# Layer 0's output product in a written order, with heads made ready two ahead, weights' low parts on two engines, and h scaled by its norm ahead of a plain transpose

## The chip, the cores and the metric

The kernel runs on one core of one Trainium2 chip. The metric is the device time of one execution in microseconds (us); the time of a kernel is the median of its runs. Five engines work side by side, each through its own instructions in order: TensorE (PE, with its weight loads PEld), VectorE (DVE), ScalarE (ACT), GpSimd (POOL) and SyncE (SP), which issues nearly all transfers. Engines wait for each other through semaphores. Matrix products are made by PE from on-chip memory (SBUF) into PSUM; DVE and ACT read both, POOL is used on SBUF alone.

## The reference

The model has two layers over 256 context tokens and 512 latent tokens of width 1024. Layer 0 mixes by a bidirectional gated delta rule with 16 value heads of width 128, layer 1 by grouped-query attention. What the change touches is the end of layer 0, the gated residual, and the norm ahead of layer 1:

```python
def finish(o, z):
    b, h, l, dv = o.shape
    o = rms_norm(jnp.transpose(o, (0, 2, 1, 3)), o_norm_g).astype(z.dtype)
    return (o.reshape(b, l, DN_VAL_DIM) * jax.nn.silu(z)) @ w_out
...
        h_lat = h_lat + gate[:, None] * y_lat
        if need_ctx:
            h_ctx = h_ctx + gate_c * y_ctx
...
        u_lat = rms_norm(h_lat, norm_g[i]) * (1.0 + scale[:, None]) + shift[:, None]
        u_ctx = rms_norm(h_ctx, norm_g[i]) * (1.0 + scale_c) + shift_c
```

Here `rms_norm(x, g)` is x over the root of the mean of its squares (plus 1e-6), times g.

## The kernel before

**Tiles.** The 768 tokens are six tiles of 128 rows: 0 and 1 the context, 2 to 5 the latents. Layer 0 leaves the mixer's result in `O[t]`, one tile of 128 x 16 x 128 for each token tile. Products are made with operands split in two: a high part rounded to the matrix engine's fp32r and a low part, the rest. Each product is three matmuls (`PASS`: high by high, high by low, low by high). The high part of a weight or an activation is a copy by ACT, the low part a subtraction by DVE or POOL.

**The scan.** Layer 0's recurrence takes some 50 steps x, which end shortly before 791 us. Beside its last steps run small pieces of work: `square_o` sums the squares of a head of `O[t]` on ACT, and `scale_pieces` makes the reciprocal root from them on DVE in pieces between steps (by a shift, a magic constant and three Newton steps) and then scales `O[t]` on POOL, four heads an instruction (L863). Tiles 0, 1 and 5 are treated so.

**The output product.** `out_group(gi)` runs twice. Group 0 has the token tiles 0, 1, 5, group 1 the tiles 4, 3, 2 (`GROUPS`). A group runs over the 16 heads, so there are 32 units. `out_prep` makes a head ready: it loads the 128 rows of `w_out` of the head (L870), copies the high part on ACT (L871), subtracts the low part on POOL as one 128x1024 instruction (L872), loads the gate z, transposes the three tiles of `O` on PE (L895), multiplies by z and the norm's weight on DVE (L898), and makes the high part y on ACT (L900) and the low part on DVE (L901). The unit is then 3 tiles x 2 halves x 3 passes = 18 matmuls of 128x512 (L1138) that add up over the heads in six PSUM tiles `po`. `out_prep` of a head is written one unit ahead of its products. The pool `fw` has two buffers for w, wh, wl, z and y.

In group 0, at heads 2, 5 and 8, the squares and the scale of the tiles 4, 3, 2 are made: 16 `square_o` on ACT and `scale_o`, whose last instruction scales a whole tile on POOL (L827). In group 1, at heads 3, 5, 7 and 9, the key/value weights of layer 1 (`wkv`) are loaded and split.

**The end of a group.** For each of its three tiles and two halves DVE multiplies the sum by the gate (`gy`, L1143, four buffers), POOL adds it to `h_t` (L1144), and ACT sums the squares (L1145). `norms1` makes the reciprocal root on DVE and from it, on ACT, a diagonal matrix `diag1[t]` (L1167). `u_block(k, ...)` turns block k of 128 columns: a matmul of `h_t` with the diagonal (L1174) transposes and scales in one, DVE applies the affine map of layer 1 (L1176), ACT and DVE make the two parts (L1177, L1178). `u_block` for the context is written beside `kv_block` (L1240), the key/value products, for the latents behind it.

**What sets the order.** Up to this point a scheduler orders the instructions of each engine from the program, from priorities and from when it thinks operands are ready; `issue_after` keeps an instruction behind a named one. From the blocks of the latents on (`manual_schedule`) PE, DVE and ACT run in the order in which the code is written; POOL and SP stay with the scheduler.

## Time and profile before

| | |
|---|---|
| time, median of 3 runs | 1297.53 us (1296.28 to 1298.45) |
| the profiled execution: its own time | 1297.93 us |
| the profiled execution: span from first to last instruction | 1296.2 us |
| mean granted TensorE clock | 0.966 of full speed |
| first and last product of the output stage (L1138) | 791.0 and 959.7 us |
| its 576 matmuls, in 32 units | 18 each |
| first and last `u_block` matmul (L1174) | 950.3 and 1001.8 us |

All times in the trace are of one profiled execution, counted from the first instruction. A row of a timeline gives start, duration, engine, line, operation, tiles and shape; in brackets stands the idle time of the engine ahead of the instruction and what ended it. A row of one line's summary gives the shortest, median and longest duration in ns and the first and last start. Matmuls are pipelined, so their durations overlap and the distance from one start to the next is what one costs.

### The profile page before, as it was taken

Reading aid. Unit: us, or ns where it says so; the run is one execution under the profiler, and the core shown is the slowest. Engines: PE = TensorE matmul, PEld = TensorE weight load, DVE = VectorE, ACT = ScalarE, POOL = GpSimd, SP = SyncE. Lnnn points to the kernel's source line nnn. Section 1 sums busy time; section 2 is a strip of 40 time slices with the busy share of each in tenths; the row PEclk is TensorE's granted clock in tenths of the full one; section 3 lists DMA queues with packets and bytes.
Section 4 is the critical chain, followed back from the end, with each engine's and each line's share of the span. In section 5 each row is a group of like instructions: output and inputs, shape, how many; then the busy total and the mean of one; then the engine's idle time right before and its main releaser. Section 6 shows DMA issues by size and latency. Waiting matters only on the chain.

```text
span 1296.2 us, 28116 instructions
## 1 busy us (share of the span) xinstructions
PE 1170.6 (90%) x10803; PEld 940.9 (73%) x10803; DVE 822.0 (63%) x1800; ACT 705.3 (54%) x1892; POOL 641.8 (50%) x503
## 2 busy tenths in 40 slices
PE   3999999999789898999999988897999787989996
PEld 1676778888678777887666655685787677878874
DVE  2688566777897466765888884754346456555535
ACT  3344336665476768963898874633332244545621
POOL 0121132169989998302665785675662234331540
PEclk9999999999899988999999999998999988989998
DMA  9366976355545597539799666454642021010233
GB/s 315 130 220 206 327 245 169 113 167 167 151 123 184 154 269 239 180 125 283 235 247 246 166 181 172 152 166 134 186 133 66 1 65 50 17 34 33 66 98 97
DMA packets 165351, 204.56 MB, mean 158 GB/s; under 512 B 13377, under 2 KB 114914, under 8 KB 164322
## 3 DMA queue, kind: packets, MB, share of 16 engines
q1 hardware_dynamic: 146402, 193.33, 49.0%
q10 hardware_dynamic: 18816, 9.44, 2.5%
q8 instruction: 85, 1.39, 0.4%
q14 instruction: 48, 0.39, 0.1%
HBM read 161.96 MB, written 40.67 MB: 156 GB/s over the span
## 4 chain that ended last, share of the span: by engine, by line
PE 54%; DVE 14%; POOL 9%; DMA 9%; ACT 8%; issue 4%; SPq 1%; ACTq 0%; DVEq 0%; POOLq 0%
PE ks L979 6%; PE g_q L335 5%; PE po L1138 5%; PE g_v L335 4%; PE g_z L335 4%; PE pg L1348 3%; PE su L1034 3%; PE po L1426 2%; PE g_k L335 2%; PE pg L1371 2%; PE pr L1004 2%; POOL wol L872 2%; POOL X L677 2%; PE pso L1445 2%; POOL tmp L676 2%
## 5 line engine op out<-in xcount | busy, mean ns | idle before, releaser
L987 POOL TENSOR_TENSOR S<-S,glb 128x512 f32<-128x512 f32 x88 | 90.1, 1047 | 112.5 <-PE ks L979 112.4
L1138 PE MATMUL po<-woh,y 128*128 128x512 f32 x384 | 127.8, 403 | 11.1 <-ACT y L900 8.3
L335 PE MATMUL g_v<-uh,wh 128*128 128x512 f32 (+1 forms) x256 | 91.5, 357 | 15.7 <-DVE sil_v L362 15.7
L872 POOL TENSOR_TENSOR wol<-wo,woh 128x1024 fp32r<-128x1024 f32 x32 | 76.3, 2390 | 52.7 <-ACT woh L871 52.4
L677 POOL TENSOR_TENSOR X<-X,tmp 128x62 f32<-128x62 f32 (+15 forms) x93 | 96.8, 1040 | 6.5
L979 PE MATMUL ks<-S,ckq 128*64 128x256 f32 x768 | 93.5, 385 | 3.4 <-ACT o L984 2.7
L357 DVE SCALAR_TENSOR_TENSOR acc_v<-g_v,cwv,acc_v 128x510 f32<-128x510 f32 (+3 forms) x128 | 74.4, 609 | 34.7 <-ACT acc_v L354 33.2
L335 PE MATMUL g_z<-uh,wh 128*128 128x512 f32 (+1 forms) x256 | 88.9, 347 | 4.6 <-DVE sil_v L362 4.5
L676 POOL TENSOR_TENSOR tmp<-L,X 128x62 f32<-128x62 f32 (+15 forms) x93 | 89.1, 958 | 6.9
L1138 PEld LDWEIGHTS po<-woh,y 128*128 128x128 f32 x384 | 71.6, 191 | 27.7 <-ACT y L900 9.2
L335 PE MATMUL g_v<-ul,wh 128*128 128x512 f32 (+1 forms) x256 | 90.0, 352 | 0.0
L335 PE MATMUL g_v<-uh,wl 128*128 128x512 f32 (+1 forms) x256 | 89.2, 349 | 0.0
L335 PE MATMUL g_z<-ul,wh 128*128 128x512 f32 (+1 forms) x256 | 87.4, 342 | 0.0
L335 PE MATMUL g_z<-uh,wl 128*128 128x512 f32 (+1 forms) x256 | 87.3, 341 | 0.0
L979 PEld LDWEIGHTS ks<-S,ckq 128*64 128x64 f32 x768 | 50.7, 136 | 42.6 <-ACT o L984 11.7
L1138 PE MATMUL po<-wol,y 128*128 128x512 f32 x192 | 77.6, 404 | 4.0 <-POOL wol L872 4.0
L317 POOL TENSOR_TENSOR wl_k<-w_k,wh_k 128x1024 fp32r<-128x1024 f32 x8 | 19.0, 2386 | 101.8 <-ACT wh_k L316 101.8
L335 PEld LDWEIGHTS g_v<-uh,wh 128*128 128x128 f32 x256 | 50.8, 198 | 22.5 <-DVE sil_v L362 16.4
L1397 ACT ACTIVATE pr<-s,nm,sq 128x768 f32<-128x768 f32 x32 | 31.8, 993 | 62.9 <-DVE nm L1394 62.4
L1348 PE MATMUL pg<-wq,uL 128*128 128x256 f32 x384 | 56.0, 293 | 5.0 <-ACT qj L1357 2.6
L1052 DVE TENSOR_TENSOR S<-su,S 128x512 f32<-128x512 f32 x88 | 56.5, 683 | 4.1 <-PE su L1034 2.9
L982 DVE SCALAR_TENSOR_TENSOR r<-ks,negV,cv 128x128 f32<-128x128 f32 x192 | 56.1, 343 | 3.3 <-PE ks L979 2.5
(370 smaller groups left out, 3384.6 us busy)
## 6 DMA issues: line engine op xcount, KB each, us to landing
aw<-in_ada_w SPq DMA_DIRECT2D x24, 1024.0 KB, 7.8
w<-in_dn_w_in SPq DMA_DIRECT2D x40, 512.0 KB, 4.4
wo<-in_dn_w_out SPq DMA_DIRECT2D x32, 512.0 KB, 3.3
cv<-v_d SPq DMA_DIRECT2D x80, 128.0 KB, 5.3
df<-gc_d SPq DMA_DIRECT2D x48, 128.0 KB, 2.8
z_d<-zs SPq DMA_DIRECT2D x16, 384.0 KB, 4.9
v_d<-vt ACTq DMA_DIRECT2D x16, 384.0 KB, 3.9
t_d<-Tt SPq DMA_DIRECT2D x6, 1024.0 KB, 4.8
```

The lines of the kernel that those rows point to most:

```text
L335: mm = T.matmul(pg_[:m, :n], w[:, k, :m], u[:, k, c0:c0 + n], start=k == 0 and n_ == 0, stop=k == KT - 1 and n_ == 2)
L357: V.scalar_tensor_tensor(acc[:, c0 + lo:c0 + hi], ps[:, lo + j - 2:hi + j - 2], cwv[:, j, ct:ct + 1], acc[:, c0 + lo:c0 + hi], ALU.mult, A ...
L676: E.tensor_tensor(tv, bcast(L[:, :, j + 1:, j], 3, j + 1), bcast(X[:, :, j, 0:j + 1], 2, n), ALU.mult)
L677: E.tensor_tensor(X[:, :, j + 1:, 0:j + 1], X[:, :, j + 1:, 0:j + 1], tv, ALU.subtract)
L872: G.tensor_tensor(wl, w, wh, ALU.subtract)
L979: T.matmul(ks[r0:r0 + 64, w], kq[:, w, slot(hh), r0:r0 + 64], St[hh][:, d], start=True, stop=True)
L982: V.scalar_tensor_tensor(r[:, 2 * j + i], ks[:, 0, i], negV[:, visit, t, h0 + i:h0 + i + 1], v[:, 2 * hh + i], ALU.mult, ALU.add)
L987: G.tensor_tensor(St[hh], St[hh], bcast(g_, 3, P), ALU.mult)
L1034: T.matmul(su[c0:c0 + 64, d ^ j, j], kt[r0:r0 + 64, 4 * j + p, c0:c0 + 64], vd[r0:r0 + 64, 2 * j:2 * j + 2], start=True, stop=True)
L1052: V.tensor_tensor(St[hh], raw(sj, 0, [[512 - 1024 * j, 2], [P, 2], [1, P]]), St[hh], ALU.add)
L1138: T.matmul(acc[j][nh], y[i][:, j, :], ww[k][:, nh * 512:(nh + 1) * 512], start=h == 0 and x == 0, stop=h == VH - 1 and x == 2)
L1348: T.matmul(pgq, uL[i][:, k, t * P:(t + 1) * P], wq[j][:, k], start=k == 0 and n_ == 0, stop=k == KT - 1 and n_ == 2)
```

## The change

From the output stage on, PE, DVE and ACT run in the written order (`manual_schedule` now opens ahead of the 32 units). The loop over the units `n` does, in this order: load z of head n+3 (three buffers); make y of head n+2 ready (three buffers); up to three pieces of `scale_pieces` for the tiles 4, 3, 2, which begin at the units 4, 7 and 10 and use the unused quarter of the transposes' PSUM tile; five squares of `O` on ACT until the 48 are done (units 0 to 9); in unit 20 the norm of group 0, in units 21 to 23 the scaling of its h by ACT, and from unit 24 on one context `u_block` in each; then the 18 products; the gated products at a group's end (`gy` with six buffers); in unit 4 the loads of h for group 0 and of the gate, in unit 10 those of h for group 1, each behind the next head's weight load; then the weights of head n+2, whose low part is now two halves of 512 columns, one by POOL and one by DVE; two additions to h in each of the units 16, 17 and 18; and the key/value weights as before.

`h_t` is now scaled in place by its norm, and `u_block` is a transpose with the identity in place of a product with a diagonal. At the end of group 1 POOL adds one half of each tile and DVE the other; the 8 context `kv_block` stand together, then the norm, then the scaling of tile 4 on ACT, tile 3 on DVE and tile 2 on ACT. `scale_o` is gone. In `scale_pieces`, which the scan uses too, the result of the shift is written to PSUM and no longer to SBUF.

```diff
-        V.tensor_single_scalar(y.bitcast(I32), f.bitcast(I32), 1, ALU.logical_shift_right)
-        V.tensor_scalar(y.bitcast(I32), y.bitcast(I32), -1.0, float(0x5F3759DF), ALU.mult, ALU.add)
+        V.tensor_single_scalar(sp.bitcast(I32), f.bitcast(I32), 1, ALU.logical_shift_right)
+        V.tensor_scalar(y.bitcast(I32), sp.bitcast(I32), -1.0, float(0x5F3759DF), ALU.mult, ALU.add)
...
+    def out_weights(n, shared=True):
...
         S.copy(wh, w)
-        G.tensor_tensor(wl, w, wh, ALU.subtract)
-        return wh, wl
+        c = 512 if shared else D
+        G.tensor_tensor(wl[:, :c], w[:, :c], wh[:, :c], ALU.subtract)
+        if shared:
+            V.tensor_tensor(wl[:, c:], w[:, c:], wh[:, c:], ALU.subtract)
+        weights[n] = wh, wl
...
+    def added(t, nh, gy, E):
+
+        c = slice(nh * 512, (nh + 1) * 512)
+        E.tensor_tensor(h_t[t][:, c], h_t[t][:, c], gy, ALU.add)
+        S.activation(gy, h_t[t][:, c], AF.Square, accum_out=hsq[:, ORDER.index(t), nh:nh + 1])
+        if t >= 2 and nh == 1:
+            dma(h_d[t - 2], h_t[t])
...
+    def normed(t, E):
+
+        r = hr[:, ORDER.index(t):ORDER.index(t) + 1]
+        if E is S:
+            S.activation(h_t[t], h_t[t], AF.Copy, scale=r)
+        else:
+            E.tensor_scalar(h_t[t], h_t[t], r, None, ALU.mult)
...
         for q, t in enumerate(tiles):
-            T.matmul(ps[:, q, :], h_t[t][:, k * P:(k + 1) * P], diag1[t], start=True, stop=True)
+            T.transpose(ps[:, q, :], h_t[t][:, k * P:(k + 1) * P], ident)
...
+    for n in range(len(units0)):
+        gi, h = units0[n]
...
+        if n + 3 < len(units0):
+            out_z(n + 3)
+        pt = out_y(n + 2) if n + 2 < len(units0) else None
+        for x in [x for x in chores if x <= n]:
+            for _ in range(3):
+                try:
+                    chores[x].send(pt[:, 3])
...
+        for t, h_ in squares[:5]:
+            square_o(t, h_)
+        squares = squares[5:]
+        if n == 20:
+            norms1(0, (pt[:, 3, 0:3], pt[:, 3, 64:67]))
+        if n in (21, 22, 23):
+            normed(ORDER[n - 21], S)
+        if n >= 24:
+            u_block(n - 24, 1, (0, 1), uC)
+        products0(n, acc)
+        if h == VH - 1:
+            late_adds = gated(gi, acc)
+        if n in (4, 10):
+            with tc.issue_after(w_at[n + 1]):
+                load_h(n // 10)
+                if n == 4:
+                    dma(gate0, gate_d[0])
+        if n + 2 < len(units0):
+            out_weights(n + 2)
+        if n in (16, 17, 18):
+            for x in range(2):
+                added(*late_adds.pop(0), G)
...
     for k in range(KT):
-        u_block(k, 1, (0, 1), uC)
         kv_block(k, (0, 1))
-    norms1((2, 3, 4, 5), "l")
-    manual = ExitStack()
-    manual.enter_context(tc.manual_schedule(engines={T.engine, V.engine, S.engine}))
+    norms1(1, room("hl", 3))
+    for t, E in ((4, S), (3, V), (2, S)):
+        normed(t, E)
```

What this moves on the engines is shown at three places. A name ends in a number that is the program's own count; `y_7_0` is the high or low part of y made for head 7 of group 0, `woh` and `wol` are the weight's two parts, `pt` the transposed tiles.

The first is DVE in group 0, in the middle of the norm of one tile of `O`. Before, with `fo` and `rs` (both in SBUF) as its scratch:

```order
L901 TENSOR_TENSOR y_7_0_10623<-pt_0_10615,y_7_0_10622 128x384
L898 SCALAR_TENSOR_TENSOR pt_0_10653<-pt_0_10653,og,z_0_10650 128x128 x2
L824 TENSOR_TENSOR fo<-oss,or_7093 128x16
L174 TENSOR_SCALAR fo<-fo 128x16
L175 TENSOR_SCALAR rs_12_10572<-fo 128x16
L185 TENSOR_SCALAR rs_12_10572<-rs_12_10572 128x16
L188 SCALAR_TENSOR_TENSOR rs_12_10573<-rs_12_10572 128x16
L189 TENSOR_TENSOR rs_12_10573<-rs_12_10573,fo 128x16
```

After, one unit there, from the low part of y to DVE's half of the weight's low part:

```order
L902 TENSOR_TENSOR y_9_0_10672<-pt_0_10664,y_9_0_10671 128x384
L847 TENSOR_SCALAR pt_0_10664<-oy 128x16
L848 TENSOR_TENSOR fo<-pt_0_10664,rq 128x16
L828 COPY pt_0_10664<-oss 128x16
L829 TENSOR_TENSOR pt_0_10664<-pt_0_10664,rq 128x16
L830 COPY ow<-pt_0_10664 128x16
L832 COPY pt_0_10664<-ow 128x16
L833 TENSOR_TENSOR pt_0_10664<-pt_0_10664,rq 128x16
L834 TENSOR_SCALAR fo<-pt_0_10664 128x16
L836 TENSOR_SCALAR pt_0_10664<-fo 128x16
L837 TENSOR_SCALAR oy<-pt_0_10664 128x16
L867 TENSOR_TENSOR wol_0_10714<-wo_0_10712,woh_0_10713 128x512
```

The small steps now go in pieces through PSUM (`pt`), each in a fixed place behind the low part of y, and a 128x512 subtraction closes the unit on DVE.

The second place is POOL at the switch of the groups. Before:

```order
L872 TENSOR_TENSOR wol_1_10984<-wo_1_10982,woh_1_10983 128x1024
L1144 TENSOR_TENSOR h_10293<-h_10293,gy_0_11020 128x512
L1144 TENSOR_TENSOR h_10293<-h_10293,gy_1_11024 128x512
L1144 TENSOR_TENSOR h_10294<-h_10294,gy_0_11028 128x512
L1144 TENSOR_TENSOR h_10294<-h_10294,gy_1_11032 128x512
L872 TENSOR_TENSOR wol_1_11081<-wo_1_11079,woh_1_11080 128x1024
L1144 TENSOR_TENSOR h_10298<-h_10298,gy_0_11036 128x512
L1144 TENSOR_TENSOR h_10298<-h_10298,gy_1_11040 128x512
L872 TENSOR_TENSOR wol_1_11119<-wo_1_11117,woh_1_11118 128x1024
```

After:

```order
L865 TENSOR_TENSOR wol_1_11051<-wo_1_11049,woh_1_11050 128x512
L1136 TENSOR_TENSOR h_10293<-h_10293,gy_0_11088 128x512
L865 TENSOR_TENSOR wol_1_11102<-wo_1_11100,woh_1_11101 128x512
L1136 TENSOR_TENSOR h_10293<-h_10293,gy_1_11090 128x512
L1136 TENSOR_TENSOR h_10294<-h_10294,gy_0_11092 128x512
L1136 TENSOR_TENSOR h_10294<-h_10294,gy_1_11094 128x512
L1136 TENSOR_TENSOR h_10298<-h_10298,gy_0_11096 128x512
L1136 TENSOR_TENSOR h_10298<-h_10298,gy_1_11098 128x512
L865 TENSOR_TENSOR wol_1_11147<-wo_1_11145,woh_1_11146 128x512
```

The three weights are those of heads 0, 1 and 2 of group 1 (units 16, 17, 18). The second moved ahead of all additions but one; five additions now stand between it and the third.

The third place is ACT at the same switch. Before:

```order
L1145 ACTIVATE gy_0_11020,hsq<-h_10293 128x512
L1145 ACTIVATE gy_1_11024,hsq<-h_10293 128x512
L1145 ACTIVATE gy_0_11028,hsq<-h_10294 128x512
L871 CAST woh_1_11118<-wo_1_11117 128x1024
L1145 ACTIVATE gy_1_11032,hsq<-h_10294 128x512
L1145 ACTIVATE gy_0_11036,hsq<-h_10298 128x512
L900 CAST y_1_1_11095<-pt_1_11088 128x384
L1145 ACTIVATE gy_1_11040,hsq<-h_10298 128x512
```

After:

```order
L901 CAST y_1_1_11066<-pt_1_11059 128x384
L863 CAST woh_1_11101<-wo_1_11100 128x1024
L901 CAST y_2_1_11123<-pt_1_11116 128x384
L863 CAST woh_1_11146<-wo_1_11145 128x1024
L1137 ACTIVATE gy_0_11088,hsq<-h_10293 128x512
L1137 ACTIVATE gy_1_11090,hsq<-h_10293 128x512
L901 CAST y_3_1_11166<-pt_1_11159 128x384
L863 CAST woh_1_11189<-wo_1_11188 128x1024
```

The y of unit 17 (`y_1_1`) stood behind five squares of h; now it and the y and weight of unit 18 stand ahead of the first square.

More of the change, by code (lines that the diff above doesn't have):

```diff
@@ L881, in backbone, with out_z, out_y @@
     units0 = [(gi, h) for gi in range(2) for h in range(VH)]
-    ready, first_w = {}, {}
-    def out_prep(gi, h, pt=None):
-        wh, wl = first_w.pop(h) if gi == 0 and h < 2 else out_weights(gi, h)
-        z = fw.tile([P, 3 * P], F32, tag="z", name=f"z{h}_{gi}")
+    ys, weights, zs, w_at = {}, {}, {}, {}
+    def out_z(n):
+        gi, h = units0[n]
+        z = fw.tile([P, 3 * P], F32, tag="z", name=f"z{h}_{gi}", bufs=3)
         c = 0
-        for c0, n in ZCOLS[gi]:
-            dma(z[:, c:c + n], z_d[h, :, c0:c0 + n])
-            c += n
+        for c0, m in ZCOLS[gi]:
+            dma(z[:, c:c + m], z_d[h, :, c0:c0 + m])
+            c += m
+        zs[n] = z
+    def out_y(n, pt=None):
+        gi, h = units0[n]
+        z = zs.pop(n)
         if pt is None:
@@ L898, in out_prep @@
             V.scalar_tensor_tensor(pj, pj, og, raw(z, off, [[st_, 2], [1, 64]]), ALU.mult, ALU.mult)
-        y = [fw.tile([P, 3, P], F32R, tag=f"y{i}", name=f"y{i}_{h}_{gi}") for i in range(2)]
-        ready["copy"] = S.copy(y[0], pt[:, :3]).ins
+        y = [fw.tile([P, 3, P], F32R, tag=f"y{i}", name=f"y{i}_{h}_{gi}", bufs=3) for i in range(2)]
+        S.copy(y[0], pt[:, :3])
         V.tensor_tensor(y[1], pt[:, :3], y[0], ALU.subtract)
-        ready[gi, h] = y, (wh, wl)
+        ys[n] = y
+        return pt
     with tc.tile_pool(name="psC", bufs=2, space=PSUM, reuse_waits="tile") as pcx:
@@ L1075, in backbone @@
                 if x in (45, 46):
[L1076 removed]
+                    out_weights(x - 45, False)
+                    out_z(x - 45)
         for _, g_ in chores:
@@ L1099, in backbone @@
     gate0 = fw.tile([P, 2, D], F32, tag="gate0", name="gate0", bufs=1)
-    with tc.issue_after(mark[1]):
-        dma(gate0, gate_d[0])
     def room(nm, n):
@@ L1139, in out_group, with products0, gated @@
+    ORDER = [t for g_ in GROUPS for t, _, _ in g_]
+    def products0(n, acc):
+        gi, h = units0[n]
+        y, ww = ys.pop(n), weights.pop(n)
+        for j in range(3):
+            for nh in range(2):
+                for x, (i, k) in enumerate(PASS):
+                    T.matmul(acc[j][nh], y[i][:, j, :], ww[k][:, nh * 512:(nh + 1) * 512], start=h == 0 and x == 0, stop=h == VH - 1 and x == 2)
+    def gated(gi, acc):
+        out_ = []
         for j, (t, _, _) in enumerate(GROUPS[gi]):
@@ L1178, in u_block @@
         V.tensor_tensor(dst[1][:, k], pv, dst[0][:, k], ALU.subtract)
-    with tc.issue_after(mark[0]), tc.issue_after(mark[1]):
-        load_h(0)
-    out_group(0)
-    norms1((0, 1), "c")
-    load_h(1)
-    out_group(1)
+    manual = ExitStack()
+    manual.enter_context(tc.manual_schedule(engines={T.engine, V.engine, S.engine}))
+    with tc.issue_after(mark[1]):
+        out_z(2)
+    chores = {4: scale_pieces(4, 1), 7: scale_pieces(3, 1), 10: scale_pieces(2, 1)}
+    for g_ in chores.values():
+        next(g_)
@@ new lines, in backbone @@
+    squares = [(t, h) for t in (4, 3, 2) for h in range(VH)]
+    late_adds = []
+    for n in range(len(units0)):
+        gi, h = units0[n]
+        if h == 0:
+            acc = [[pf.tile([P, 512], F32, tag=f"po{j}{nh}", name=f"po{gi}{j}{nh}") for nh in range(2)] for j in range(3)]
+        if n + 3 < len(units0):
[5 more added lines that the diff above has]
+                    chores[x].send(pt[:, 3])
+                except StopIteration:
+                    chores.pop(x)
+                    break
+        for t, h_ in squares[:5]:
[20 more added lines that the diff above has]
+                added(*late_adds.pop(0), G)
+        if gi == 1 and h in (3, 5, 7, 9):
+            k0 = h - 3
+            w = fw.tile([P, D], F32, tag="w", name=f"w1kv_{k0}")
+            wv = w.rearrange("p (k n) -> p k n", n=512)
+            dma(wv, wa[:, k0:k0 + 2, 1024:1536])
+            S.copy(wkv[0][:, k0:k0 + 2], wv)
+            G.tensor_tensor(wkv[1][:, k0:k0 + 2], wv, wkv[0][:, k0:k0 + 2], ALU.subtract)
@@ L1186, in backbone @@
+    for t, nh, gy in late_adds:
+        added(t, nh, gy, G if nh == 0 else V)
     opool_x = [fw_c, opool_c, gates_c]
```

63 lines of the change are left out of this document (10 added, 53 removed).

## The prediction

> **What bounds the kernel now.** I read the page first, then a table of the output stage by stretches, then TensorE's timeline at the places where that table shows little work, and last the lines of the engines that TensorE waits for there. The page's first part (engine, busy us, share of the span, instructions) and its groups (line, operation, busy us and mean ns of one, then idle time ahead of it and its releaser) say:
>
> ```profile
> PE 1170.6 (90%) x10803; PEld 940.9 (73%) x10803; DVE 822.0 (63%) x1800; ACT 705.3 (54%) x1892; POOL 641.8 (50%) x503
> L1138 PE MATMUL po<-woh,y 128*128 128x512 f32 x384 | 127.8, 403 | 11.1 <-ACT y L900 8.3
> L872 POOL TENSOR_TENSOR wol<-wo,woh 128x1024 fp32r<-128x1024 f32 x32 | 76.3, 2390 | 52.7 <-ACT woh L871 52.4
> ```
>
> TensorE is the bound overall. In the output products it loses 11.1 us ahead of one group alone, 8.3 of them to one ACT copy. The stage by stretches (from:to, length, then busy us of PE, PEld, DVE, ACT, POOL, the granted clock, DMA share, GB/s): group 0, the switch of the groups, what follows it, the rest of group 1, and the way to the first turned block of the latents:
>
> ```profile
> 791.00:876.40 85.40, 77.85 (x352) 61.66 (x353) 45.66 (x114) 39.29 (x134) 52.06 (x23) 0.99 0.61 173
> 876.40:883.80 7.40, 0.45 (x5) 0.21 (x3) 5.11 (x16) 2.95 (x7) 7.15 (x5) 0.81 0.21 71
> 883.80:888.30 4.50, 4.50 (x12) 3.54 (x13) 1.08 (x5) 1.24 (x4) 0.00 (x0) 0.55 0.78 267
> 888.30:960.10 71.80, 67.70 (x316) 54.21 (x315) 26.85 (x66) 24.84 (x35) 42.28 (x19) 1.00 0.46 144
> 960.10:974.90 14.80, 13.61 (x69) 11.08 (x68) 8.82 (x29) 6.63 (x20) 12.81 (x9) 1.00 0.65 213
> ```
>
> TensorE's timeline gives the price of a head that waits for nothing, between two rows that each open one, and the hole at the switch:
>
> ```profile
> 845.01 0.49 PE L895 MATMUL pt<-ident,O 128*128 128x128 f32 x3
> ...
> 849.48 0.49 PE L895 MATMUL pt<-ident,O 128*128 128x128 f32 x3
> ...
> 876.34 0.49 PE L895 MATMUL pt<-ident,O 128*128 128x128 f32 x3
> 883.78 0.80 PE L1138 MATMUL po<-woh,y 128*128 128x512 f32 x1 [6.95 <-ACT y L900]
> ```
>
> A head costs 849.48 - 845.01 = 4.47 us: 18 products of 128x512 at about .23 (18 x .23 = 4.1) and three transposes. Sixteen cost 71.5. Group 0 took 85.4, so 13.9 are lost in it. The switch loses 7.4 us, and behind it 12 products took 4.50 at a granted clock of .55 in place of 12 x .23 = 2.7: another 1.8. Group 1 took 4.50 + 71.80 = 76.3; less that 1.8 it is 74.5, 3.0 over its sixteen heads, some of which is the first turned blocks. ACT's timeline says why the hole ends when it does:
>
> ```profile
> 883.25 0.48 ACT L900 CAST y<-pt 128x384 fp32r<-128x384 f32 x1 [2.46 <-DVE roomhc L181]
> ```
>
> The copy that head 17 needs stands on ACT behind squares and behind the norm that DVE was making, work with later use.
>
> **The change part by part.** *The scan.* One integer shift now writes PSUM in place of SBUF. A starved instance of its neighbour and TensorE's steps around it:
>
> ```profile
> 768.51 3.13 DVE L845 TENSOR_SCALAR oy<-fo 128x16 int32<-128x16 int32 x1
> ```
>
> ```profile
> 764.79 1.95 PE L979 MATMUL ks<-S,ckq 128*64 128x256 f32 x16
> ...
> 768.56 1.95 PE L979 MATMUL ks<-S,ckq 128*64 128x256 f32 x16
> ...
> 774.36 1.95 PE L979 MATMUL ks<-S,ckq 128*64 128x256 f32 x16
> ```
>
> One step lasted 3.77, the next 5.80. I take the whole difference, **-2.0**. The ends are -3 (the 3.13 and no more) and 0 (the next operation with an SBUF target stalls instead).
>
> *Group 0.* These rows price the work around the products (shortest, median, longest ns of one):
>
> ```profile
> L898 DVE SCALAR_TENSOR_TENSOR pt<-pt,og,z x96: 344/359/361, 789.2 to 947.6; 128x128 f32<-128x128 f32 x96
> L900 ACT CAST y<-pt x32: 456/479/482, 790.4 to 950.3; 128x384 fp32r<-128x384 f32 x32
> L901 DVE TENSOR_TENSOR y<-pt,y x32: 545/558/559, 790.9 to 950.8; 128x384 fp32r<-128x384 f32 x32
> L818 ACT ACTIVATE ojk<-O x96: 292/295/314, 643.3 to 842.3; 128x128 f32<-128x128 f32 x96
> L871 ACT CAST woh<-wo x32: 1037/1050/1089, 779.0 to 950.7; 128x1024 fp32r<-128x1024 f32 x32
> L317 DVE TENSOR_TENSOR wl_ab<-w_ab,wh_ab x1: 685/685/685, 32.0 to 32.0; 128x512 fp32r<-128x512 f32 x1
> L863 POOL TENSOR_TENSOR O<-O,fo x12: 1043/1052/1057, 737.7 to 790.6; 128x512 f32<-128x512 f32 x12
> ```
>
> In the written order the engines pass the work round a ring: DVE multiplies three tiles (3 x .359 = 1.08), ACT copies (.48), makes five squares (5 x .295 = 1.48) and the weight's high part (1.05), DVE its half of the low part (.69, by the 128x512 row), and only then comes DVE's next head. With some .17 for four hand-overs that is 4.95, over the 4.47 of TensorE. Ten units hold squares: 10 x .48 = 4.8. With two heads ready in place of one, most of a head is in hand at the start, so I take 2.0 (ends 0 and 4.8). POOL scales each of the three tiles with four instructions in a row, 4 x 1.05 = 4.2. The weight behind them waits: its place comes free when the products of the head two before end, after which it needs 1.05 on ACT and about 1.2 on POOL (half of 2.39), 2.3 of the 4.47, so 2.2 are slack and each batch may cost 4.2 - 2.2 = 2.0. For three batches I take 5.0 (ends 0 and 6). Loading h for three tiles and the gate, 2.5 MB, now starts in unit 4; at the 173 GB/s of this stretch it takes 14.5 us beside the weights. I take 1.0; the ends are 0 and 4, a little under one head. So 71.5 + 8.0 = 79.5 in place of 85.4, **-5.9** (ends -13.9 and +1).
>
> *The switch.* Copies of heads 17 and 18 now stand ahead of the squares and the norm of group 0 on ACT, and the six gated products have six buffers, so none waits for a square. What is late next is the weight of head 18: on POOL five additions stand ahead of it.
>
> ```profile
> L1144 POOL TENSOR_TENSOR h<-h,gy x12: 1275/1311/1332, 871.4 to 964.8; 128x512 f32<-128x512 f32 x12
> ```
>
> The additions that stand together take 5 x 1.31 = 6.6. TensorE has head 17 to do in that time and part of head 16, 4.47 and more. I count 1.3 left of the 7.4 (ends 0 and 6.6 - 4.47 = 2.1) and no slow products behind it: 7.4 + 1.8 - 1.3 = **-7.9** (ends -9.2 and -5.3, the latter if the slow clock comes back too). By the Trainium skill (TensorE: Matmul & The Clock Gate, Part 1: The HAM clock gate) the rate falls to half after an idle window of about 3.4 us; this trace has .55 behind 7.4 us, no run here shows a gap of 1 to 4 us, and by that figure the 1.8 would come back only past 3.4.
>
> *Group 1.* Heads 21 to 23 carry the scaling of h by ACT, at about the 1.05 of a 128x1024 copy, and two of them a layer-1 weight of another 1.05 as well: ring 1.08 + .48 + 1.05 + 1.05 + 1.05 + .69 + .17 = 5.6, 1.1 over a head, twice, less what is in hand: 1.5. From head 24 on a block of the context is turned in each:
>
> ```profile
> L1177 ACT CAST uC<-ht x8: 353/373/375, 951.8 to 972.9; 128x256 fp32r<-128x256 f32 x8
> L1178 DVE TENSOR_TENSOR uC<-ht,uC x8: 411/424/425, 952.2 to 973.3; 128x256 fp32r<-128x256 f32 x8
> ```
>
> The ring there is 1.08 + .48 + .56 + .55 (the affine step, by L901's time for 128x384) + .37 + 1.05 + .69 + .2 = 5.0. TensorE's own is 4.47 plus two transposes of .11, 4.69; six such heads lose 6 x .3 = 1.8, counted as 1.7. Then 71.5 + 8 x .22 + 1.5 + 1.7 = 76.5 in place of 74.5: **+2.0** (ends -1.2, all hidden, and +4).
>
> *The tail.* The context's blocks are done by then, so 48 key/value products stand alone ahead of the latents: 48 x .23 = 11.0. Beside them runs the chain of the last additions, squares, norm and scaling. The row that opens the norm now:
>
> ```profile
> 966.94 0.42 DVE L1164 TENSOR_TENSOR hrl<-hsq 128x4 f32<-128x4 f32 x1 [3.54 <-ACT gy L1145]
> ```
>
> Three additions move to DVE (about .69 each), so the sum of squares comes some 3 us earlier than 966.94, which is 6.8 behind the end of the products; the norm's fifteen small steps are no longer mixed with the context's blocks; two scalings on ACT take 2 x 1.05. Undisturbed the chain ends near 9.4 and the products decide, at 11.0. But POOL splits layer 1's weights beside it, in steps of up to 2.4. Two such blocks of DVE make 9.4 + 4.8 = 14.2; three make it 16.6. I take 14.3 in place of 14.8, **-.5** (ends -3.8 and +1.8).
>
> *The latents' blocks.* The product with a diagonal is now a plain transpose:
>
> ```profile
> L1174 PE MATMUL ht<-dn,h x96: 270/275/347, 950.3 to 1001.8; 128*128 128x128 f32 x96
> L895 PE MATMUL pt<-ident,O x96: 270/272/421, 787.0 to 946.0; 128*128 128x128 f32 x96
> ```
>
> The code has 8 x 2 + 8 x 4 = 48 products with a diagonal, and the trace 96 records: two passes each. It has 32 x 3 = 96 transposes and 96 records: one pass. A block of four tiles drops four passes of .11, .44, where TensorE runs without a pause:
>
> ```profile
> 984.34 1.05 PE L1174 MATMUL ht<-dn,h 128*128 128x128 f32 x8
> ...
> 988.04 1.05 PE L1174 MATMUL ht<-dn,h 128*128 128x128 f32 x8
> ```
>
> A block's pitch is 3.70. Seven intervals save 7 x .44 = **-3.1** (ends -3.1 and 0, if DVE's and ACT's part decides instead).
>
> Sum: -2.0 - 5.9 - 7.9 + 2.0 - .5 - 3.1 = -17.4. The profiled execution took 1297.93, .4 above the median of the runs shown; 1297.93 - 17.4 = 1280.5, and by the median 1280.1: **1280**.
>
> **The rivals.** *A, slower.* The weight's low part is now made by POOL and DVE at once, right behind ACT's high part, and those two engines block each other. The trace has this in group 0:
>
> ```profile
> 816.58 2.40 POOL L872 TENSOR_TENSOR wol<-wo,woh 128x1024 fp32r<-128x1024 f32 x1 [0.68 <-ACT woh L871]
> 816.59 2.42 DVE L188 SCALAR_TENSOR_TENSOR rs<-rs 128x16 f32<-128x16 f32 x1
> ```
>
> POOL started .01 us earlier, and DVE's operation on sixteen columns took as long as POOL's whole subtraction. If POOL's half starts first in each head, DVE's waits 1.2 more and every ring grows by it: with squares 6.15, so 10 x 1.68 = 16.8 where 2.0 stands; eleven plain heads go from 3.5 to 4.7, 11 x .23 = 2.5; the three with scaling grow by 4.4, the six with blocks by 6 x 1.2 = 7.2. That is +28.9: 1309. It decides from the point where POOL is first in three heads of five (17.4 / 28.9). Against it speak DVE's low parts of layer 0's other weights, made while POOL had work of its own:
> ```profile
> L317 DVE TENSOR_TENSOR wl<-w,wh x32: 1172/1295/3358, 235.9 to 581.6; 128x1024 fp32r<-128x1024 f32 x32
> ```
>
> Half of the 32 took 1.30 or less where the quickest took 1.17: the long ones are few. Chance .08. The Trainium skill (SBUF — State Buffer, SBUF: two separate sides) has the rule that whichever of the two starts first holds the shared port pair for its whole instruction; by it the split saves only where DVE wins or the two are apart, and this row agrees with it.
>
> *B, more is gained.* The spare heads swallow the ring's and POOL's delays. Then group 0 loses 1.0 (-12.9), the switch nothing (-9.2), group 1 nothing (-1.2), the tail is 11.0 (-3.8), scan and transposes as above (-5.1): -32.2, **1266**. For it: rings that pass 4.47 stand in bunches with plain heads between. Against it: weights still have two buffers, so only y is two ahead. Chance .27.
>
> *C, the change doesn't do what it says.* The heads stand ready, but the weights are the late part and remain one ahead. Group 0 keeps its 13.9, and the moved load costs 4 more; the rest stays: -2.0 + 4.0 - 7.9 + 2.0 - .5 - 3.1 = -7.5, **1290**. The 52.4 us that POOL waits for L871 speak against it: it is idle, not late. Chance .15.
>
> *D, no net change.* The waits of the switch and of group 0 come back as waits for weights, 17.4 / 32 = .54 in each head: about 1297. Against it: POOL's 52.4 idle us. Chance .05.
>
> **How the numbers follow.** My forecast, with its own range 1274 to 1287, has .45, B .27, C .15, D .05, A .08. The range goes from 1267, which leaves out B's lower part, to 1293, which takes in C and leaves out A and D; some 2 in 10 lie beyond it. A measurement of this kernel can tell about .2%, 2.6 us, from no change. Faster: .45 + .27 + .15 = .87; the same .05; slower .08.
>
> **What would show it.** After the change TensorE's holes of over 3 us inside the output stage should be gone, and the clock in the ten us after the switch be near 1. Units 0 to 9 should show a pitch of 4.5 to 5, with pauses of about 2 behind POOL's four scalings; DVE's 128x512 low parts should take .69, and 1.2 to 1.9 would be rival A. The turned blocks should have half the records and a pitch near 3.26. The step of the scan at 768 should last 3.8. I am wrong if the weights' low part releases most of TensorE's waits, or if the tail grows past 16.

## The result, and the profile after

The changed kernel took **1305.59 us** (median of 6 runs) beside 1297.96 for the kernel before (6 runs): a ratio of 1.0052, with a 95% interval of 1.0028 to 1.0077. In a later measurement the same program took 1299.09 (12 runs) beside 1298.91 (29 runs), 1.0005 (0.9989 to 1.0022). The change gained nothing and cost up to half a per cent, where 17 us less were forecast.

Two lines of the page after answer to those of before, and a third to the weights' low part:

```profile
PE 1174.3 (90%) x10755; PEld 943.3 (72%) x10755; DVE 847.0 (65%) x1864; ACT 707.6 (54%) x1891; POOL 618.5 (47%) x509
L1120 PE MATMUL po<-woh,y 128*128 128x512 f32 x384 | 132.2, 413 | 3.0 <-ACT woh L863 3.0
L865 POOL TENSOR_TENSOR wol<-wo,woh 128x512 fp32r<-128x512 f32 (+1 forms) x32 | 54.9, 1714 | 80.2 <-ACT woh L863 70.5
```

TensorE's wait for y is gone from the second line (8.3 us before), and yet the products' busy time rose from 127.8 to 132.2: they ran slower. The stage by stretches after (from:to, length, busy us of PE, PEld, DVE, ACT, POOL, granted clock, DMA share, GB/s) is units 0 to 15, 16 and 17, 18 to 31, the way to the first block of the latents, and these blocks:

```profile
792.40:881.60 89.20, 78.14 (x335) 62.41 (x335) 51.66 (x159) 36.88 (x128) 37.18 (x27) 0.92 0.57 171
881.60:890.80 9.20, 9.17 (x43) 7.35 (x42) 8.13 (x13) 3.72 (x7) 8.70 (x7) 1.00 0.48 153
890.80:966.80 76.00, 67.22 (x306) 53.40 (x305) 42.80 (x102) 32.42 (x51) 36.62 (x21) 0.98 0.46 144
966.80:982.80 16.00, 10.86 (x48) 8.66 (x48) 11.85 (x22) 5.39 (x13) 10.70 (x9) 0.93 0.68 229
982.80:1015.80 33.00, 30.53 (x132) 24.01 (x133) 19.27 (x47) 8.63 (x31) 4.58 (x2) 0.88 0.11 33
```

The hole of 7.4 us at the switch is gone: units 16 and 17 take 9.2, close to 2 x 4.47, at full clock. But units 0 to 15 take 89.2 where 16 x 4.47 is 71.5, and the other four stretches run below full clock. TensorE's timeline shows the new holes (in brackets the idle time ahead of the row and its releaser):

```profile
823.86 0.79 PE L1120 MATMUL po<-woh,y 128*128 128x512 f32 x1 [2.73 <-ACT woh L863]
825.71 0.79 PE L1120 MATMUL po<-wol,y 128*128 128x512 f32 x1 [1.05 <-POOL wol L865]
...
871.49 0.47 PE L896 MATMUL pt<-ident,O 128*128 128x128 f32 x1 [4.46 <-POOL O L854]
...
893.08 0.50 PE L1120 MATMUL po<-wol,y 128*128 128x512 f32 x1 [1.54 <-POOL wol L865]
...
925.34 0.42 PE L1171 MATMUL ht<-ident,h 128*128 128x128 f32 x2 [3.29 <-issue]
...
982.82 1.94 PE L1171 MATMUL ht<-ident,h 128*128 128x128 f32 x8 [5.16 <-POOL wz L1254]
```

The length of a unit is read from the row of its first transposes to that of the next unit's. In the changed kernel units 1 to 5, 7, 8, 10, 11, 13, 15, 17, 19 and 20 take 4.45 to 4.47; what is lost is in unit 0 (6.4 us, its first products at a granted clock of .50), 6 (11.2), 9 (5.8), 12 (6.8), 14 (10.5), 18 (6.3), and in 21 to 28, above all 24 (9.8).

**Unit 6.** What TensorE waits for at 823.86 is read on ACT:

```profile
822.77 1.04 ACT L863 CAST woh<-wo 128x1024 fp32r<-128x1024 f32 x1 [5.03 <-DMA wo<-in_dn_w_out]
```

and the queue of loads shows what stood ahead of that weight:

```profile
808.33 1.75 SPq L1147 DMA_DIRECT2D h<-in_ctx  x3
810.12 1.23 SPq L1147 DMA_DIRECT2D h<-in_x  x2
811.42 0.57 SPq L1216 DMA_DIRECT2D gate<-gate_d  x1
812.16 0.34 SPq L862 DMA_DIRECT2D wo<-in_dn_w_out  x1
```

ACT could begin on the weight issued at 812.16, right behind them, only 10.6 later; the page gives 3.4 from issue to landing as the median of all 32. The 2.5 MB of h and gate were still under way: by the trace the last part of h landed at 818.0 and the gate at 820.8. The weight of unit 12, issued behind the h of group 1, made ACT wait 3.7 in the same way.

**Unit 14.** Its third transpose, at 871.49, waits for POOL's scaling of tile 2. The last small step on DVE and POOL's scaling are these:

```profile
868.49 0.17 DVE L848 TENSOR_TENSOR fo<-pt,rq 128x16 f32<-128x16 f32 x1
```

```profile
868.67 1.77 POOL L865 TENSOR_TENSOR wol<-wo,woh 128x512 fp32r<-128x512 f32 x1 [3.23 <-DVE fo L848]
870.40 4.03 POOL L854 TENSOR_TENSOR O<-O,fo 128x512 f32<-128x512 f32 x4
```

The step is written in unit 13, but DVE runs late and reaches it 1.8 us into unit 14 (which begins at 866.65); then a weight's low part, ready at the same moment, goes ahead of the scaling on POOL.

**Units 21 to 28.** The loaded weights have two buffers, and the key/value weights of layer 1 use them too. The rows of the weight of unit 24: POOL's last use of the buffer that it takes (the low part of unit 23's weight), its load, ACT's copy, and DVE behind it:

```profile
915.74 1.78 POOL L865 TENSOR_TENSOR wol<-wo,woh 128x512 fp32r<-128x512 f32 x1 [4.95 <-ACT woh L863]
```

```profile
917.55 0.33 SPq L862 DMA_DIRECT2D wo<-in_dn_w_out  x1
```

```profile
921.25 1.05 ACT L863 CAST woh<-wo 128x1024 fp32r<-128x1024 f32 x1 [2.19 <-DMA wo<-in_dn_w_out]
```

```profile
922.33 0.69 DVE L867 TENSOR_TENSOR wol<-wo,woh 128x512 fp32r<-128x512 f32 x1 [3.72 <-ACT woh L863]
...
924.68 0.56 DVE L902 TENSOR_TENSOR y<-pt,y 128x384 fp32r<-128x384 f32 x1 [0.60 <-ACT y L901]
```

The load is issued .03 after POOL lets go of the buffer (915.74 + 1.78 = 917.52), since a key/value weight holds the other one, and ACT and, in its written order, DVE stand until it lands. From there on DVE is late, and TensorE reaches the first turned block while its PSUM tile is still in use: DVE's low part of y, which frees it, ends at 925.24, and the block's transposes start at 925.34. (The timeline names no releaser there; the shared tile is read from the program.)

**The tail.** DVE's first steps of the last norm, and POOL beside them:

```profile
972.37 0.74 DVE L1155 TENSOR_TENSOR hr<-hsq 128x3 f32<-128x3 f32 x1 [2.04 <-ACT gy L1137]
973.14 2.33 DVE L174 TENSOR_SCALAR hr<-hr 128x3 f32<-128x3 f32 x1
975.51 2.32 DVE L175 TENSOR_SCALAR rs<-hr 128x3 int32<-128x3 int32 x1
977.87 0.17 DVE L178 TENSOR_SCALAR roomhl<-rs 128x3 int32<-128x3 int32 x1
```

```profile
973.06 2.39 POOL L1255 TENSOR_TENSOR wz<-w1z,wz 128x1024 fp32r<-128x1024 f32 x1
975.41 2.39 POOL L1255 TENSOR_TENSOR wq<-w1q,wq 128x1024 fp32r<-128x1024 f32 x1
```

Two operations on three columns end with two whole subtractions of POOL; the next one, which writes PSUM, takes .17.

### The profile page after: what moved, and what is told of

The parts are those of the page before. It is cut to its first block, busy times and chain, and to the rows that moved or that the text cites. A ratio compares the mean times of both kernels' runs of the same rounds, so it can differ in the third digit from the quotient of the medians.

```text
span 1304.7 us, 28127 instructions
## 1 busy us (share of the span) xinstructions
PE 1174.3 (90%) x10755; PEld 943.3 (72%) x10755; DVE 847.0 (65%) x1864; ACT 707.6 (54%) x1891; POOL 618.5 (47%) x509
## 4 chain that ended last, share of the span: by engine, by line
PE 52%; DVE 15%; DMA 10%; POOL 9%; ACT 8%; issue 4%; SPq 1%; ACTq 0%; DVEq 0%; POOLq 0%
PE ks L981 6%; PE g_z L335 5%; PE g_q L335 4%; PE po L1120 4%; PE pg L1392 3%; PE su L1036 3%; PE g_v L335 3%; PE po L1470 2%; PE pg L1415 2%; PE g_k L335 2%; DMA wo<-in_dn_w_out 2%; POOL X L677 2%; PE pr L1006 2%; POOL tmp L676 2%; PE pso L1489 2%
## 5 line engine op out<-in xcount | busy, mean ns | idle before, releaser
L1120 PE MATMUL po<-woh,y 128*128 128x512 f32 x384 | 132.2, 413 | 3.0 <-ACT woh L863 3.0
L865 POOL TENSOR_TENSOR wol<-wo,woh 128x512 fp32r<-128x512 f32 (+1 forms) x32 | 54.9, 1714 | 80.2 <-ACT woh L863 70.5
L1120 PEld LDWEIGHTS po<-woh,y 128*128 128x128 f32 x384 | 75.8, 197 | 19.3 <-ACT woh L863 3.5
L1441 ACT ACTIVATE pr<-s,nm,sq 128x768 f32<-128x768 f32 x32 | 31.8, 993 | 62.7 <-DVE nm L1438 62.2
```

The costliest lines, as they stand in the source:

```text
L865: G.tensor_tensor(wl[:, :c], w[:, :c], wh[:, :c], ALU.subtract)
L1120: T.matmul(acc[j][nh], y[i][:, j, :], ww[k][:, nh * 512:(nh + 1) * 512], start=h == 0 and x == 0, stop=h == VH - 1 and x == 2)
```

## The experiments

All but two start from the changed kernel. The table has, in us and from each kernel's one profile: the output stage (first product to the end of the last), the way from there to the first key/value product of the latents, from there to layer 1's first gate product (z, which two expectations call the query product), some units, and units 24 to 28 together; then the median and the ratio to the kernel before on the same chip.

| kernel | stage | to kv | to z | 6 | 9 | 12 | 14 | 18 | 24-28 | median | ratio (95%) |
|---|---|---|---|---|---|---|---|---|---|---|---|
| before | 169.1 | 17.4 | 30.1 | | | | | | | 1297.96 | |
| before_again | 169.3 | 17.4 | 30.1 | | | | | | | 1299.37 | 1.0009 (0.9991-1.0027) |
| after | 174.3 | 18.7 | 30.4 | 11.2 | 5.8 | 6.8 | 10.5 | 6.3 | 31.6 | 1305.59 | 1.0052 (1.0028-1.0077) |
| after_again | 172.9 | 18.6 | 30.8 | 8.3 | 7.2 | 6.8 | 10.7 | 6.3 | 31.1 | 1299.09 | 1.0005 (0.9989-1.0022) |
| e1_loads | 170.6 | 18.8 | 29.7 | 4.5 | 8.9 | 5.6 | 11.2 | 6.3 | 31.2 | 1297.11 | 0.9987 (0.9972-1.0003) |
| e2_scale | 166.2 | 18.7 | 29.6 | 9.5 | 4.5 | 4.5 | 4.5 | 6.2 | 30.9 | 1296.07 | 0.9980 (0.9958-1.0002) |
| e3_pool_low | 170.2 | 18.6 | 30.8 | 11.1 | 5.3 | 8.1 | 4.6 | 4.5 | 30.4 | 1293.08 | 0.9965 (0.9946-0.9984) |
| e4_norm_psum | 174.1 | 13.8 | 28.4 | 9.2 | 6.5 | 8.3 | 10.1 | 6.3 | 31.8 | 1293.45 | 0.9971 (0.9954-0.9989) |
| e6_ulate | 170.9 | 21.6 | 30.5 | 8.0 | 7.3 | 5.8 | 11.4 | 6.3 | 30.0 | 1304.58 | 1.0040 (1.0024-1.0055) |
| e7_low_last | 176.7 | 19.5 | 29.6 | 6.4 | 5.5 | 8.5 | 12.2 | 4.5 | 32.1 | 1304.28 | 1.0044 (1.0028-1.0061) |
| e8_w3 | 165.3 | 18.8 | 30.5 | 4.4 | 8.9 | 5.6 | 11.0 | 6.3 | 26.4 | 1291.32 | 0.9950 (0.9933-0.9967) |
| best1 | 163.3 | 18.1 | 28.4 | 4.5 | 4.8 | 5.7 | 5.7 | 4.5 | 33.2 | 1288.78 | 0.9923 (0.9900-0.9945) |
| best2 | 153.5 | 15.0 | 29.7 | 4.5 | 4.7 | 5.7 | 5.7 | 4.5 | 24.7 | 1276.16 | 0.9834 (0.9820-0.9849) |
| best3 | 157.9 | 13.9 | 28.4 | 4.5 | 4.5 | 4.5 | 4.5 | 6.3 | 26.3 | 1277.50 | 0.9843 (0.9828-0.9857) |

The medians hold more than the stages do: the first product stands at 786 to 796 us in these profiles, in programs that differ up to there by no more than the scan's shift. So single edits are read by the stages, and the medians decide only where they are far apart.

**Both kernels again.**

> The kernel before itself, on the chip of the next three, for a second profile of it. Theory (the stages ahead of the output product differ by several us between executions of one program, and what the change does is in the stages behind it): its first product stands anywhere from 786 to 796 us, while from its first product to the layer-1 query product it takes 216.6 again, within 2. Rival (the 216.6 was itself a chance value): off by more than 3.

> The changed kernel itself, once more, on the chip that the next three kernels run on. Its lead over the kernel before in the ten us around unit 0 differs between executions of one program (the first product stood at 787 to 792 us in five programs that are the same up to there). Theory (the change costs a few us by its own stalls and some of the 7.6 us was the spread of the earlier stages): 0 to 5 us slower than the kernel before; first product to the layer-1 query product 223 us, within 4. Rival (it costs 7 to 8 us): slower by 7 or more again.

From its first product to layer 1's z the kernel before took 216.6 and 216.8, the changed one 223.4 and 222.3. Ahead of it, the scan's first product (start of the first, start of the last) in the four profiles, before twice and after twice:

```profile
L979 PE MATMUL ks<-S,ckq x768: 379/379/431, 603.1 to 783.7; 128*64 128x256 f32 x192
```

```profile
L979 PE MATMUL ks<-S,ckq x768: 378/379/634, 606.1 to 788.3; 128*64 128x256 f32 x192
```

```profile
L981 PE MATMUL ks<-S,ckq x768: 379/379/431, 605.8 to 784.0; 128*64 128x256 f32 x192
```

```profile
L981 PE MATMUL ks<-S,ckq x768: 379/379/431, 599.6 to 777.9; 128*64 128x256 f32 x192
```

The stages that the change doesn't touch end, and the scan begins, 599.6 to 606.1 us in. The theory held: about 6 us of loss from the first product on (5.5 to 6.8) are the change's own. That the two ratios differ by half a per cent fits the spread ahead of it, which no run isolates; what causes the spread stays open.

**The bulk loads.** One load of 256 or 512 KB a unit, from unit 1 on:

```diff
-        if n in (4, 10):
-            with tc.issue_after(w_at[n + 1]):
-                load_h(n // 10)
-                if n == 4:
-                    dma(gate0, gate_d[0])
+        if 1 <= n < 1 + len(late_loads):
+            with tc.issue_after(w_at[n + 1]):
+                late_loads[n - 1]()
```

> The changed kernel, with h, the gate and the h of group 1 loaded in single parts of 256 to 512 KB, one a unit from unit 1 on, in place of 2.5 MB at once in unit 4 and 1.5 MB in unit 10. Theory (the bulk load holds up the weights behind it): ACT's wait of 5.0 us for wo before unit 6 goes, unit 6 comes down from 11.2 us to about 4.5, unit 12 from 6.8 to 5.8 or less, in all 7 to 9 us. Rival (the weights are late because their buffers come free late): unit 6 stays above 9 and the time within 2 us.

Unit 6 fell to 4.5, unit 12 to 5.6: the theory held for these units. The 7 to 9 us in all did not come: the stage gained only 3.7 on the changed kernel, since the next delay moved in. Unit 9 rose to 8.9, as TensorE now came early enough to find POOL busy with tile 4's scaling, and unit 14 to 11.2.

**The pieces of the scale.** `range(3)` pieces a unit became `range(4)`.

> The changed kernel, with four pieces of the scale's small steps in a unit in place of three, so each tile's scaling on POOL is released one unit earlier. Theory (tile 2 is scaled too late for the first transposes of group 1): the wait of 4.5 us before the third transpose of unit 14 goes with the slow products behind it, unit 14 comes down from 10.5 us to 4.5 to 5.5, and some 1 to 2 come back elsewhere where POOL's four instructions stand ahead of a weight: 4 to 6 us less. Rival (POOL is late there because of its other work): unit 14 stays above 8.

Unit 14 fell from 10.5 to 4.5: the last of the three tiles had been scaled too late for the transposes of head 16, which stand two units ahead of its products; now its scaling begins 3.1 us into unit 13, not 3.7 into unit 14. Units 9 and 12 fell too and unit 8 rose to 9.3, again for a weight behind four scalings. 8.1 less in the stage, more than expected.

**The low part on POOL alone.** `out_weights(n + 2, False)`:

> The changed kernel, with the whole low part of each weight on POOL, as before the change. Theory (POOL's half waits for DVE's, so the two make the low part in 1.8 us after the high part where one engine needs 2.4): units without another delay stay at 4.5; those that wait for wol (units 6, 9, 12, 18, 23) grow by about 0.6 each, and DVE gets 0.7 a unit back in units 24 to 28: together within 3 us of the changed kernel, more likely slower. Rival (DVE and POOL blocking each other is what cost the change its gain): 8 us or more faster.

Neither as expected nor the rival: the stage is 4.1 shorter than the changed kernel's, and unit 14 alone 5.9 shorter (10.5 to 4.6). Without its half DVE reached tile 2's last small step 3.1 us into unit 13, and the scheduler put the scaling behind 15 weights on POOL in place of 16. Outside unit 14 the stage is 1.8 longer; units 12 and 17 (8.5) rose. What the split alone is worth stays open, since POOL's order changed with it. The rows of the changed kernel show how little it can be in one unit; DVE's half, POOL's half beside it, and a half of POOL's with no other beside it:

```profile
813.95 0.69 DVE L867 TENSOR_TENSOR wol<-wo,woh 128x512 fp32r<-128x512 f32 x1 [1.85 <-ACT woh L863]
```

```profile
814.00 1.80 POOL L865 TENSOR_TENSOR wol<-wo,woh 128x512 fp32r<-128x512 f32 x1 [2.96 <-ACT woh L863]
...
909.50 1.28 POOL L865 TENSOR_TENSOR wol<-wo,woh 128x512 fp32r<-128x512 f32 x1 [1.11 <-ACT woh L863]
```

DVE starts .05 earlier, and POOL's half takes 1.80 in place of 1.28. The low part is whole at 815.80, some .6 earlier than one subtraction of 2.40 would have made it.

**The last norm.** Its sum, shift and next step go through PSUM:

```diff
-        V.tensor_tensor(r, hsq[:, 3 * gi:3 * gi + 3, 0], hsq[:, 3 * gi:3 * gi + 3, 1], ALU.add)
-        rsqrt(r, 1.0 / D, room=room_)
+        V.tensor_copy(yp, hsq[:, 3 * gi:3 * gi + 3, 0])
+        V.tensor_tensor(yp, yp, hsq[:, 3 * gi:3 * gi + 3, 1], ALU.add)
+        V.tensor_scalar(r, yp, 1.0 / D, EPS, ALU.mult, ALU.add)
+        V.tensor_single_scalar(yp.bitcast(I32), r.bitcast(I32), 1, ALU.logical_shift_right)
...
```

> The changed kernel, with the norm's first steps written to PSUM, or reading from it, in place of SBUF alone. Theory (DVE's small steps of the last norm stand behind POOL's splits of layer 1's weights, 0.7 + 2.3 + 2.3 us): these three fall to some 0.2 each, the first block of the latents starts within 12 us of the last product in place of 16.2, the twelve key/value products behind it take 3.0 to 3.5 in place of 5.4; 5 to 7 us less. Rival (the rows are long because DVE waits for data): the chain keeps its length and the time stays within 1.5 us.

```profile
967.19 0.16 DVE L1159 TENSOR_SCALAR hr<-roomhl 128x3 f32<-128x3 f32 x1
967.38 0.17 DVE L1160 TENSOR_SCALAR roomhl<-hr 128x3 int32<-128x3 int32 x1
...
968.79 0.17 DVE L1164 SCALAR_TENSOR_TENSOR roomhl<-roomhl,hy 128x3 f32<-128x3 f32 x1
...
970.27 2.73 DVE L1174 TENSOR_SCALAR h<-h,hr 128x1024 f32<-128x1024 f32 x1
```

```profile
967.69 2.39 POOL L1265 TENSOR_TENSOR wz<-w1z,wz 128x1024 fp32r<-128x1024 f32 x1
```

The steps of 2.33 and 2.32 take .16 and .17 beside a copy by POOL (1.04 from 966.69), and those beside its subtraction no more. The way to the latents' products falls from 18.7 to 13.8, and the stretch behind it by 2.0: 6.9 together, as expected. One operation from SBUF to SBUF is left there: DVE's scaling of tile 3 takes 2.73 beside POOL's next subtraction, and .75 in the changed kernel.

**The turned blocks behind the products.** The two lines of `u_block(n - 24, ...)` after `products0(n, acc)`:

> The changed kernel, with the context's turned block of units 24 to 31 written behind the unit's products in place of ahead of them. Theory (TensorE stands before the block's transposes with products ready behind them, since DVE and ACT run late by the norm, the scaling of h and weights that landed late): units 24 to 28 come down from 31.6 us together to 24 to 26. Rival (the weights of those units are late anyway): they stay above 29, and the tail grows by what the last block now takes.

The rival: units 24 to 28 took 30.0, and the tail grew by 2.9. TensorE's place in line was not what was late.

**The low parts last.** `for xs in ((0, 2), (1,))` around the products, so that the pass that reads the weight's low part comes last:

> The changed kernel, with the six products that read a weight's low part at the end of each unit in place of every third product. Theory (POOL's scalings and additions stand ahead of the low parts, which a unit reads with its second product): the low part is needed 2.7 us later, TensorE's waits for wol in units 6, 9, 12, 18 and 23 (1.1, 1.1, 1.5, 1.5, 0.8) go; units 9, 18 and 23 take 4.5 to 4.7. In all 4 to 6 us less. Rival (the order of passes changes nothing, as the high part or y is as late): the same units stay within 0.5 of what they took.

Half held: unit 18 fell from 6.3 to 4.5, unit 23 from 5.5 to 4.5. But units 12, 14, 21 and 24 took 8.5, 12.2, 7.1 and 11.7, each for a load, a scaling or the norm that TensorE now reached earlier; without unit 0 the stage is 168.2, as in the changed kernel (168.4), so the 4 to 6 us did not come.

**Three buffers for loaded weights.** `bufs=3` for the tiles `w`:

> The changed kernel, with three buffers in place of two for the weights as they are loaded (the key/value weights of layer 1 share them). Theory (in units 19 to 28 three loads pass through two buffers in two units, so a weight's load is issued only when POOL has split the key/value weight, and lands late): TensorE's losses in units 21 to 28 (some 10 us over 4.47 a unit, and .22 where a block is turned) fall to 5 or less, and unit 6 falls too, since the weight is loaded a unit earlier, to 4.5 to 7. 6 to 10 us less in the output stage. Rival (the norm on DVE and the scaling of h on ACT make these units late): units 21 to 28 lose 8 or more still.

ACT's copies of the weight by what they waited for, in the changed kernel and here:

```profile
L863 ACT CAST woh<-wo 128x1024 fp32r<-128x1024 f32 x32 | 33.5, 1048 | 24.8 <-DMA wo<-in_dn_w_out 16.9 <-PE po L1120 5.5 <-PE ht L1171 1.4
```

```profile
L863 ACT CAST woh<-wo 128x1024 fp32r<-128x1024 f32 x32 | 33.5, 1047 | 16.9 <-PE po L1120 13.2 <-issue 3.4 <-DMA wo<-in_dn_w_out 0.4
```

The 16.9 us for loads fell to .4, units 24 to 28 from 31.6 to 26.4 (5 x 4.69 = 23.5 would be no loss), unit 6 to 4.4. The stage is 9.0 shorter. This was the theory, against the norm and the scaling of h. Two things it had otherwise: 8.8 of the 16.9 were the waits of units 6 and 12 behind the bulk loads, and the load that ACT waited for before unit 24 came behind a weight's own low part. In unit 6 the bulk still delays the weight here (issued at 804.91, copied from 814.33), but the issue is early enough to hide it.

**Together.** The first combination has the single loads, four pieces, the norm through PSUM, the blocks behind the products and the low parts last; the second has three buffers and leaves the blocks ahead of the products; the third is the second with the low parts' products in their old places.

> The changed kernel with five edits at once: single loads, four pieces a unit, the last norm through PSUM, the turned blocks behind the products, and the low parts' products last. If each theory holds and the delays don't take each other's place: output stage 150 to 154 us in place of 174 (32 x 4.47 = 143 is the floor without the turned blocks, 145 with them), from the last product to the latents' first key/value product 13 to 14, and about 1275 to 1280 us in all. Rival (another delay appears behind each that goes): stage above 160, time above 1284.

> The changed kernel with single loads, four pieces a unit, the last norm through PSUM, the low parts' products last, and three buffers for the loaded weights; the turned blocks stay ahead of the products. Output stage 150 to 156 us, from the last product to the latents' first key/value product 13 to 14; faster than the kernel before by 1.2 to 1.8%. Rival (delays take each other's place): stage 160 or more.

> The same as the last, with the low parts' products in their old places, every third. Theory (POOL's scalings and additions then hold up the units that read the low part early): stage 3 to 6 us longer than with the low parts last. Rival (with weights a unit earlier the low parts are early too): within 1 us of it.

The first kept 163.3 in the stage, its rival's case: units 24 to 28 took 33.2. The second came to 153.5 and to **1276.16 us, 1.7% faster than the kernel before**; its way to the latents' products, 15.0, missed the 13 to 14. It differs from the first by the third buffer and by the blocks' place; that the buffer is the main part is argued from the two single edits. The third gave 4.4 of the stage back, as expected: unit 8 took 11.5 in place of 6.9, with a hole of 4.54 for a low part behind four scalings. The stretches behind its stage are 2.3 shorter, and its 1277.50 is not clear of the second's time. The second's stretches, the same five as above:

```profile
787.20:866.40 79.20, 72.88 (x337) 57.97 (x336) 56.07 (x160) 37.41 (x129) 36.03 (x27) 1.00 0.66 195
866.40:875.70 9.30, 9.30 (x43) 7.05 (x42) 7.57 (x14) 3.17 (x8) 9.01 (x7) 1.00 0.41 140
875.70:940.80 65.10, 64.30 (x306) 52.41 (x305) 40.03 (x97) 30.71 (x48) 34.59 (x20) 1.00 0.49 160
940.80:953.60 12.80, 10.90 (x49) 8.68 (x47) 10.56 (x26) 6.09 (x14) 11.04 (x8) 1.00 0.71 246
953.60:985.40 31.80, 29.04 (x132) 22.72 (x133) 19.25 (x47) 8.68 (x31) 6.72 (x4) 0.95 0.16 50
```

What is to be seen is the clock, 1.00 up to the latents, units 0 to 15 in 79.2 us in place of 89.2, and TensorE busy for 64.3 of the 65.1 us of units 18 to 31.

## Why the prediction was wrong

Point by point, the prediction's own figure and what the changed kernel's profile showed:

| term | predicted | measured |
|---|---|---|
| scan, stalled step | -2.0 | -2.0 at the step, -1.1 up to the first product (-2.6 in the second pair of profiles) |
| lost in units 0 to 15 | 8.0 | 89.2 - 71.5 = 17.7 |
| lost at the switch (units 16 to 18) | 1.3 | .2 + 1.8 = 2.0 |
| lost in the rest of group 1 | 3.2 | 76.0 - 14 x 4.47 - 8 x .22 - 1.8 = 9.8 |
| tail to the latents' first block | 14.3 | 16.0 |
| latents' blocks | -3.1 | +.3 |

The six differences add up to some 23 us, which takes the forecast of -17.4 to +5.6; from the scan's start to layer 1's z the changed kernel's profile is 5.6 longer. The steps that failed are above all three terms on what must be ready when: the loads (1.0 for what was 6.7 in unit 6), the scaling of tile 2 (nothing for what was 6.1 in unit 14) and the weights' buffers in group 1 (3.2 for what was 9.8, and 3.8 with a third buffer).

*Right.* The scan's stalled step is gone, while one of 5.64 elsewhere stays as it was (5.66 before):

```profile
767.42 1.95 PE L981 MATMUL ks<-S,ckq 128*64 128x256 f32 x16
771.20 1.95 PE L981 MATMUL ks<-S,ckq 128*64 128x256 f32 x16
```

(.9 came back as a wait of unit 0's transposes for DVE.) The switch lost 2.0, within the forecast's ends (0 and 2.1), and for the reason given: unit 18 waits 1.54 for the weight behind five additions, at full clock. A block with plain transposes has half the records and a pitch of 3.18 (990.70 to 993.88), where 3.26 was forecast and 3.70 stood before.

*Wrong in size: the loads.* "I take 1.0; the ends are 0 and 4, a little under one head" was 6.7 in unit 6 (3.9 in the second profile, where the hole was 2.01 and full clock followed it), and part of the 2.3 in unit 12. The bytes and the rate were right; that the weight behind the bulk has little time to land, since it is issued only when one of two buffers comes free, was not counted, nor that a hole can bring slow products: 3.8 of idle time cost 6.7. The reading that no run shows a gap of 1 to 4 us was wrong, as the kernel before has holes of 3.08 (at 811.10) and 1.98 us in group 0, both followed by full clock.

*Wrong by a missing deadline: the scaling.* The sum had POOL's scalings hold up weights (5.0; in units 9 and 12 it was at most 3.6, part of it the loads) and did not ask when tile 2 must be ready. With heads made ready two ahead the transposes of head 16 stand in unit 14, and the pieces, three a unit from unit 10, are written to end in unit 13, with no time to spare when DVE runs late. That was 6.1; a piece more in each unit removed it, and so did freeing DVE of its half of the low part.

*Wrong by a queue left out: group 1.* The ring was worked out from durations alone (1.5 + 1.7). The prediction asked of each moved step what its loads do, but not how many loads pass through the two buffers in units 19 to 26: three in two units. Three buffers took away 5.2 of the 8.1 lost in units 24 to 28 (31.6 to 26.4).

*Wrong in the pieces, nearly right in the sum: the tail.* The two blocks behind POOL came as priced, 2.33 + 2.32. But the squares of h ended only some 5.6 us after the last product, not 3 earlier than before's 6.8: DVE's first addition, behind its six gated products and beside one of POOL's, took 1.53 where .69 was counted.

*Wrong by what follows a hole: the latents' blocks.* The transposes gained 1.75 us up to z, not 3.1, since one interval between blocks grew by .55. The gap of 5.2 ahead of them was followed by products at half clock (.50): the first twelve key/value products took 5.3 in place of 3.2, which ate that gain.

*Not there: the ring of units 0 to 9* (2.0): units 1 to 8 but for 6 take 4.45 to 4.47 with five squares in each.

The stretch that the prediction calls group 0 holds 17 units, not 16, so 4.5 of its 13.9 belonged to group 1's side; the sum counts each of the 32 once and is not moved by it. Of the rivals, D (no net change, about 1297, chance .05) and A (1309, chance .08) lie on either side of the two measurements. Part of D's mechanism is there: in the stage TensorE waits 5.9 us for low parts of weights and 3.0 for high parts. But these waits stand in a few units, not as .54 in each, and those for the scaling and the turned block are not in D. C had the weights late behind the loads, and the wrong depth, since it left the rest of the gains standing. A's lock was real but the other way round: DVE wins by .05 and POOL pays .5 (24 of DVE's 30 halves take about .69, and 23 of POOL's about 1.8). By the Trainium skill (SBUF — State Buffer, SBUF: two separate sides) the first to start keeps the ports for its whole instruction, which these rows agree with: POOL's half ends 1.16 after DVE's, where 1.28 is its length alone.
